# PEER's gate arrays: the one-hot arrays of the first key by eight compare-and-multiply steps on VectorE, and GpSimd as the splitter of the query blocks and the first 17 key blocks only

## The chip, the cores and the metric

The kernel runs on one core of a Trainium2 chip. The time is the device time of one execution of the whole program, in microseconds (us); the median of three runs before the change is 4424.07 us. TensorE (PE in the rows) multiplies matrices, VectorE (DVE), ScalarE (ACT) and GpSimd (POOL) work on arrays in SBUF, and SyncE (SP) issues nearly all DMAs. Each engine takes its own instructions strictly in the order in which the program put them.

## The reference

Three blocks of a network follow one another over 512 tokens of 1024 features. The change lies in the second block's expert layer, PEER. Cut to what matters:

```python
q = einsum('bsd,dk->bsk', xm, w_q).reshape(b, s, 8, 2, 128)      # 8 heads, two keys each
sc = einsum('bshpc,hpnc->bshpn', q, sub_keys)                    # scores of 2 x 128 sub-keys
top_s, top_i = top_k(sc, 16)
best_s, best_c = top_k(top_s[..., 0, :, None] + top_s[..., 1, None, :], 16)   # of 256 pairs
i1, i2 = the two sub-keys of each of the 16 best pairs
g = softmax(best_s)                                              # gates
h = gelu(xm . u[i1 * 128 + i2])                                  # u, v: 16384 x 1024
y = sum over the 8 * 16 chosen experts of g * h * v[i1 * 128 + i2]
```

## The kernel before

The kernel computes all 16384 experts for all tokens and multiplies the hidden values by a dense array of gates that is zero where an expert was not chosen. A block is 128 experts with one second key i2 each for all 128 first keys, or in the kernel's order one key block j: 128 rows of `u` and of `v`. The stage `stage_peer` goes through four stretches.

*Search.* For each of the 8 heads, two query blocks of `peer_w_q` are multiplied with the tokens (`linear`), ScalarE and TensorE make the scores, and `peer_topk` finds the 16 best pairs, all on VectorE. TensorE meanwhile also works through the first of 48 early key blocks of `peer_u` (`EARLY = 48`), whose hidden values ScalarE computes and SyncE stores to DRAM (`H_dr`).

*Gates.* `peer_gates` works on 128 tokens at a time (four times `b`). Three transposes bring i1, i2 and the gates of the chosen pairs onto partitions (`sT`). Then for 8 tokens at a time, 64 units in all, `oa` holds one-hot rows of i2 (a compare of `iot` = 0..127 with `sT`, line 1500) and `oe` one-hot rows of i1 (line 1501) times the gate (line 1502); 8 products on TensorE (line 1506) contract them into the dense gates, ScalarE copies these out of PSUM into `st` (line 1509), and every 32 tokens `st`, 2 MB, is stored to `G_dr` (line 1510). `oa` has two buffers and `oe` three; the products' results take turns in three PSUM banks. In between TensorE goes on with the early key blocks.

*Hand-over.* Key blocks 48 to 51 come next, and are the first whose hidden values are multiplied by the gates at once (`gated`, line 1578): that needs `gt`, loaded from `G_dr` after the last store of `st`. The results, split into `ph` and `pl`, are the moving side of the first products with `peer_v`.

*Groups.* 32 groups of 4 key blocks, with the products for `v` (line 1599).

All big products run in three passes on exact splits of fp32 operands (lines 271 to 273): `whi` is the weights rounded by ScalarE (line 227), `wlo` the rest, a subtraction of two arrays of 128 x 1024 (line 230), on the engine that `linear` is given as `eng`. So a key block is 24 products of 512 columns. Weights as loaded (`wraw`) have three buffers, `whi` and `wlo` two each, so ScalarE rounds block j only once TensorE is through with block j - 2. Query blocks give `wlo` to GpSimd. Of the early key blocks, j <= 20 and the even ones behind them go to GpSimd, the odd ones to VectorE (line 1565).

The order of the instructions on each engine is not the order of the source here: from the attention stage to the end of PEER a scheduler with a simulated timeline places them (`schedule_with_timeline_sim`), with durations of its own. Instructions that cannot run yet hold up all that stand behind them on their engine.

Of the kernel before, what the change touches and what calls it, by code (L numbers as in the profile page):

```python
# [18 lines left out]
OP = mybir.AluOpType  # L19
AX = mybir.AxisListType  # L20
PSUM = bass.MemoryType.PSUM
DRAM = bass.MemoryType.DRAM
# [3 lines left out]
KT = 8  # L26
# [4 lines left out]
# ---------------------------------------------------------------------------  # L31
# host side: layouts only
# ---------------------------------------------------------------------------
# [7 lines left out]
def _blocks_tok(w):  # L41
    """Blocks for products with tokens on the output partitions: [n/256, k half, 128, 4*256]."""
    k, n = w.shape
    return np.ascontiguousarray(
        w.reshape(2, 4, 128, n // 256, 256).transpose(3, 0, 2, 1, 4)
    ).reshape(n // 256, 2, 128, 1024)
# [7 lines left out]
class Layout:  # L54
    """Named columns of the packed per-feature vectors."""
# [16 lines left out]
def host_layout(i):  # L72
    a = {}
# [29 lines left out]
    # block 2  # L103
# [17 lines left out]
    # block 3  # L121
# [23 lines left out]
# ---------------------------------------------------------------------------  # L145
# device side
# ---------------------------------------------------------------------------
# [4 lines left out]
class Ctx:  # L152
# [50 lines left out]
    # -- psum ------------------------------------------------------------  # L203
    def banks(self, es, **split):
        """Share the 8 banks among tags; the tiles of one tag are handed out in order."""
# [14 lines left out]
    # -- exact operand splits ---------------------------------------------  # L220
    def split(self, hi, lo, x, scale=None, eng=None):
        """eng: the engine of lo, or the engines of hi and lo."""
# [18 lines left out]
    def weights(self, src, kt=KT, eng=None, raw=None, pool=None):  # L241
        """One block of up to 128 output columns: [128, kt, 128], split."""
# [8 lines left out]
    def fetch(self, w, blocks, more=(), own=False):  # L251
        """Weights of the first products of the next stage; those of more not split yet.

        own: in a pool of their own, which the next stage closes.
        """
# [10 lines left out]
    def passes(self, ps, terms, first=True, last=True):  # L266
        """terms: (lhs hi, lhs lo, rhs hi, rhs lo); first, last: where the accumulation group starts and ends."""
# [7 lines left out]
    def linear(self, w, blocks, xh, xl, epi, kt=KT, eng=None, front=0, tail=0):  # L275
        """outT[n, t] for each 128-column block of w; epi(j, psum); eng splits the weights.

        The first and the last blocks (front, tail) take one half of the tokens after the other.
        The last ones have epi(j, psum, tokens) and are left to the function returned, of the tokens.
        """  # L280
# [34 lines left out]
    def linear_steps(self, w, blocks, xh, xl, epi):  # L315
        """linear() in steps of KT products of a block."""
# [9 lines left out]
    def linear_tok(self, w, blocks, xh, xl, epi, eng=None):  # L326
        """out[t, n]: tokens on partitions; epi(j, t-pair, psum [128, 2, 256])."""
# [14 lines left out]
    # -- statistics over features ------------------------------------------  # L342
    def colsum(self, s):
        """Sum over partitions, on every partition."""
        ps = self.ax_ps()[:, :s.shape[1]]
        self.nc.tensor.matmul(ps, self.ones, s, start=True, stop=True)
        return ps

    def exp_ln(self, after=None):
        """Load the table set that serves both Exp and Ln."""  # L350
# [3 lines left out]
    def rsqrt(self, *args, load=True, **kw):  # L354
        """out = (scale * ps + eps) ** -0.5, or max(ps, eps) ** -0.5; one Newton step on exp(-ln/2)."""
# [26 lines left out]
    def scratch(self, k, ts, tag):  # L382
        """Room for what is worked out of tile k of x: at the end of a stage, what the stage leaves unused."""
# [13 lines left out]
    def sumsq_ps(self, ps, x, k, ts):  # L397
        """ps accumulates the sum of squares over the features of KT tiles, on every partition."""
# [10 lines left out]
    # -- the ends of stages, in steps between which the halves of the tokens take turns -------  # L409
    def rms_pre(self, g):  # L410
        """What a stage that begins with an RMS norm does with x: its split, scaled by rstd * g."""
# [11 lines left out]
    def modulate_pre(self, scale, shift):  # L423
        """What a stage that begins with a modulation does with x: the split of xt * scale + shift."""
# [10 lines left out]
    def enter(self, xt, pre):  # L435
        """The operands of a stage's first products, unless the stage before has left them."""
# [11 lines left out]
    def leave(self, xt, sums, rest, post, pre, dead, mu=None, first=()):  # L448
        """rest(tokens) and the steps of post(tokens) end a stage, pre begins the next."""
# [18 lines left out]
    def rms_post(self, y, acc, xt, g, sums=None):  # L468
        """xt += rms(y) * g; sums[tokens] = sum of squares of the new xt."""
# [23 lines left out]
class Small:  # L493
    """Arithmetic on small float32 tiles [128, 64]."""
# [85 lines left out]
GH = 8  # L580
# [7 lines left out]
def s5_tables(K, pool, R8, J8):  # L588
    """Discretised poles, their powers with the signs of each half of the partitions, B bar.

    Partitions are (h, n): h = 0 holds real parts of the states, h = 1 imaginary parts.
    """
# [6 lines left out]
    with K.tc.tile_pool(name="s5sm", bufs=1, side="right", reuse_waits="tile") as sp:  # L599
# [54 lines left out]
        # factors of one chunk for the states and for their copy with the halves swapped  # L654
# [6 lines left out]
def s5_inputs(K, u, A_dr, g0):  # L661
    """u: the inputs of the groups from g0 on, a chunk's rows on partitions."""
# [7 lines left out]
def s5_group(K, tb, p1, rot, g0, u, H, G_dr, K_dr):  # L670
    """GH groups: matrices of a chunk of 8 (inputs to states and to outputs), the states each chunk adds."""
# [44 lines left out]
def s5_chunks(K, p2, A_dr, K_dr, Y_dr):  # L716
    """The outputs from within a chunk of 8."""
# [18 lines left out]
def s5_scan(K, tb, rot, H):  # L736
    """The states before each chunk of 8, for every group."""
# [12 lines left out]
def s5_outputs(K, rot, q, H, G_dr, Y1_dr, Y_dr):  # L750
    """GO groups: what the states add to the outputs."""
# [18 lines left out]
def stage_even(K, xt):  # L770
# [9 lines left out]
    with ExitStack() as es:  # L780
# [28 lines left out]
        # conv branch  # L809
# [3 lines left out]
        def conv_pe(j, hb, c):  # L813
            """The taps as products with diagonal matrices."""
# [78 lines left out]
        # S5 branch  # L893
# [1368 lines left out]
```

## Time and profile before

| | |
|---|---|
| three runs | 4424.07 us median, 4422.52 to 4433.23 |
| profiled execution, first to last instruction | 4432.6 us |
| PE busy | 4120.0 us (93%) |
| DVE, ACT, POOL busy | 2799.4, 1756.8, 994.4 us |
| search | about 1541 to 1770 us |
| gates | about 1770 to 2082 us |
| hand-over | about 2082 to 2102 us |
| groups | from 2102 us |

The profiled execution's own time is its span, 4432.6 us; nothing outside the span is recorded for it. It is one execution, and lies near the longest of the three runs. Times in the rows below count from its first instruction. In a row of a group, "x64" is the number of instructions, then come their busy time in us, the mean ns of one, and behind the second bar the idle time of the engine just before them, with what ended it. A row of a timeline begins with the start and the duration; a number in brackets is the idle time before it. Ends of matmuls are modelled, so the step from one start to the next is a better measure of a matmul than its duration.

### The profile page before, as it was taken

Reading aid. Unit: us, or ns where it says so; the run is one execution under the profiler, and the core shown is the slowest. Engines: PE = TensorE matmul, PEld = TensorE weight load, DVE = VectorE, ACT = ScalarE, POOL = GpSimd, SP = SyncE. Lnnn points to the kernel's source line nnn. Section 1 sums busy time; section 2 is a strip of 40 time slices with the busy share of each in tenths; the row PEclk is TensorE's granted clock in tenths of the full one; section 3 lists DMA queues with packets and bytes.
Section 4 is the critical chain, followed back from the end, with each engine's and each line's share of the span. In section 5 each row is a group of like instructions: output and inputs, shape, how many; then the busy total and the mean of one; then the engine's idle time right before and its main releaser. Section 6 shows DMA issues by size and latency. Waiting matters only on the chain.

```text
span 4432.6 us, 54533 instructions
## 1 busy us (share of the span) xinstructions
PE 4120.0 (93%) x20700; PEld 3400.4 (77%) x20700; DVE 2799.4 (63%) x4731; ACT 1756.8 (40%) x2785; POOL 994.4 (22%) x827
## 2 busy tenths in 40 slices
PE   7867897999999899989999999999999999999998
PEld 5656676777776687778888888888877788877887
DVE  8999735555544699997665444444445878735334
ACT  3643634343435522334322322223264444444333
POOL 4855201111021334774000000000023222211000
PEclk9888998999999899999999999999999999999999
DMA  5543533334321123445664434333334222343322
GB/s 149 117 118 116 169 105 117 124 121 136 114 77 53 54 85 127 168 173 202 207 195 140 132 115 128 116 122 119 105 115 149 64 79 70 93 139 109 99 95 86
DMA packets 275062, 532.36 MB, mean 120 GB/s; under 512 B 75968, under 2 KB 149568, under 8 KB 271184
## 3 DMA queue, kind: packets, MB, share of 16 engines
q1 hardware_dynamic: 263328, 505.75, 35.6%
q10 hardware_dynamic: 9216, 9.97, 0.7%
q0 software_dynamic: 2256, 13.17, 0.7%
q8 instruction: 162, 2.65, 0.2%
q14 instruction: 100, 0.82, 0.1%
HBM read 438.11 MB, written 90.70 MB: 119 GB/s over the span
## 4 chain that ended last, share of the span: by engine, by line
PE 49%; DVE 14%; issue 4%; ACT 2%; DMA 2%; POOL 2%; DVEq 0%; SPq 0%; POOLq 0%; ACTq 0%
PE mm L271 14%; PE mm L272 14%; PE mm L273 14%; DVE wlo L230 1%; DVE oa L1500 1%; PE ax L1506 1%; PE z L1225 1%; DVE ti L1435 1%; DVE oe L1501 1%; POOL oe L1502 1%; PE ck L2031 1%; DVE bi L1451 1%; DVE ts L1433 1%; DMA h<-H_dr 1%; DVE wz L1983 0%
## 5 line engine op out<-in xcount | busy, mean ns | idle before, releaser
L271 PE MATMUL mm<-uh,whi 128*128 128x512 f32 (+1 forms) x2888 | 1155.3, 401 | 60.1 <-ACT whi L227 27.0
L273 PE MATMUL mm<-uh,wlo 128*128 128x512 f32 (+1 forms) x2888 | 1131.9, 392 | 53.3 <-DVE wlo L230 49.8
L272 PE MATMUL mm<-ul,whi 128*128 128x512 f32 (+1 forms) x2888 | 1132.3, 392 | 11.3 <-DVE ul L230 9.1
L227 ACT ACTIVATE whi<-wraw 128x1024 fp32r<-128x1024 f32 x455 | 480.3, 1057 | 917.5 <-PE mm L272 650.7
L230 DVE TENSOR_TENSOR wlo<-wraw,whi 128x1024 fp32r<-128x1024 f32 x399 | 515.3, 1293 | 516.5 <-ACT whi L227 504.6
L271 PEld LDWEIGHTS mm<-uh,whi 128*128 128x128 f32 x2888 | 562.8, 195 | 175.6 <-ACT whi L227 31.7
L273 PEld LDWEIGHTS mm<-uh,wlo 128*128 128x128 f32 x2888 | 562.0, 195 | 169.1 <-DVE wlo L230 57.1
L272 PEld LDWEIGHTS mm<-ul,whi 128*128 128x128 f32 x2888 | 563.1, 195 | 120.6 <-DVE ul L230 13.5
L272 PE MATMUL mm<-pl,vh 128*128 128x512 f32 (+1 forms) x1056 | 405.0, 384 | 1.4 <-DVE pl L230 1.4
L273 PE MATMUL mm<-ph,vl 128*128 128x512 f32 (+1 forms) x1056 | 397.7, 383 | 0.0
L271 PE MATMUL mm<-ph,vh 128*128 128x512 f32 (+1 forms) x1056 | 392.8, 384 | 1.9 <-ACT ph L227 1.6
L227 ACT ACTIVATE vh<-wraw 128x1024 fp32r<-128x1024 f32 x128 | 133.1, 1058 | 520.0 <-PE mm L272 320.0
L230 DVE TENSOR_TENSOR vl<-wraw,vh 128x1024 fp32r<-128x1024 f32 x128 | 155.5, 1223 | 190.3 <-ACT vh L227 190.1
L1608 POOL COPY acc<-xt 128x256 f32<-128x256 f32 x2 | 1.9, 961 | 1118.9 <-DVE xt L1606 1118.9
L1603 DVE TENSOR_TENSOR Y<-mm,Y 128x512 f32<-128x512 f32 (+1 forms) x256 | 164.1, 669 | 135.5 <-PE mm L273 135.4
L271 PEld LDWEIGHTS mm<-ph,vh 128*128 128x128 f32 x1056 | 199.2, 189 | 41.1 <-ACT ph L227 1.8
L272 PEld LDWEIGHTS mm<-pl,vh 128*128 128x128 f32 x1056 | 199.2, 189 | 40.8 <-DVE pl L230 2.1
L273 PEld LDWEIGHTS mm<-ph,vl 128*128 128x128 f32 x1056 | 199.3, 189 | 38.7
L1502 POOL TENSOR_TENSOR oe<-oe,sT 128x1024 f32<-128x1024 f32 x64 | 176.5, 2760 | 92.9 <-DVE oe L1501 58.0
L854 POOL TENSOR_TENSOR cvtp<-cvtp,cq 128x512 f32<-128x512 f32 x120 | 174.6, 1456 | 98.6 <-ACT cq L853 93.3
L230 POOL TENSOR_TENSOR wlo<-wraw,whi 128x1024 fp32r<-128x1024 f32 x56 | 154.9, 2771 | 165.7 <-ACT whi L227 165.6
L1506 PEld LDWEIGHTS ax<-oe,oa 128*128 128x128 f32 x1024 | 128.1, 195 | 45.6 <-POOL oe L1502 34.2
(1071 smaller groups left out, 7378.1 us busy)
## 6 DMA issues: line engine op xcount, KB each, us to landing
wraw<-in_peer_u_dram SPq DMA_DIRECT2D x128, 512.0 KB, 3.4
wraw<-in_peer_v_dram SPq DMA_DIRECT2D x128, 512.0 KB, 3.5
wraw<-in_w_in_f_dram SPq DMA_DIRECT2D x66, 512.0 KB, 3.3
G_dr<-st SPq DMA_DIRECT2D x16, 2048.0 KB, 7.5
gt<-G_dr SPq DMA_DIRECT2D x32, 1024.0 KB, 6.8
wraw<-in_w_ffn_dram SPq DMA_DIRECT2D x64, 512.0 KB, 3.3
wraw<-in_w_ada_dram SPq DMA_DIRECT2D x48, 512.0 KB, 3.3
wraw<-in_ev_w_in_dram SPq DMA_DIRECT2D x40, 512.0 KB, 3.4
```

The costliest lines, as they stand in the source:

```text
L227: nc.scalar.activation(out=hi, in_=x, func=AF.Copy)
L230: eng.tensor_tensor(out=lo, in0=x, in1=hi.bitcast(F32), op=OP.subtract)
L271: nc.tensor.matmul(ps, ah, bh, start=first and j == 0, stop=False)
L272: nc.tensor.matmul(ps, ah, bl, start=False, stop=False)
L273: nc.tensor.matmul(ps, al, bh, start=False, stop=last and j == n - 1)
L854: nc.gpsimd.tensor_tensor(out=c, in0=c, in1=t, op=OP.add)
L1225: nc.tensor.matmul(ps[b][:, 128 * (c - b):n], ntri if c == b else nones, at(sp, c, wide[c]), start=False, stop=c == 3, skip_group_check=True)
L1433: v.max(out=ts_[:, x, a:b], in_=src[:, x])
L1435: v.max_index(out=ti[:, x, a:b], in_max=ts_[:, x, a:b], in_values=src[:, x])
L1502: nc.gpsimd.tensor_tensor(out=e, in0=e, in1=sT[:, 2, t0:t0 + 8, None].to_broadcast(sh), op=OP.mult)
L1506: nc.tensor.matmul(pg[:, (r % 4) * 128:(r % 4 + 1) * 128], a[:, r], e[:, r], start=True, stop=True)
L1603: tt(out=Y[:, m, ts], in0=ps, in1=Y[:, m, ts], op=OP.add)
```

## The change

The compare for `oe` on VectorE and the multiplication by the gate on GpSimd, one instruction each for 8 tokens, become 8 instructions on VectorE, one for each token: each compares `iot` with the token's column of i1 and multiplies by the token's column of gates. And GpSimd splits the key blocks j < 17 only; from block 17 on every key block's `wlo` is VectorE's. Comments and docstrings are removed as well, with their lines left empty.

```diff
@@ peer_gates
-                io = iot[:, None, :].to_broadcast(sh)
-                nc.vector.tensor_tensor(out=a, in0=io, in1=sT[:, 1, t0:t0 + 8, None].to_broadcast(sh), op=OP.is_equal)
-                nc.vector.tensor_tensor(out=e, in0=io, in1=sT[:, 0, t0:t0 + 8, None].to_broadcast(sh), op=OP.is_equal)
-                nc.gpsimd.tensor_tensor(out=e, in0=e, in1=sT[:, 2, t0:t0 + 8, None].to_broadcast(sh), op=OP.mult)
+                nc.vector.tensor_tensor(out=a, in0=iot[:, None, :].to_broadcast(sh),
+                                        in1=sT[:, 1, t0:t0 + 8, None].to_broadcast(sh), op=OP.is_equal)
+                for r in range(8):
+                    t = t0 + r
+                    nc.vector.tensor_scalar(out=e[:, r], in0=iot, scalar1=sT[:, 0, t:t + 1], scalar2=sT[:, 2, t:t + 1],
+                                            op0=OP.is_equal, op1=OP.mult)
@@ stage_peer
-    EG, EARLY = 4, 48
+    EG, EARLY, SEARCH = 4, 48, 17
@@
-                         eng=nc.vector if j > 20 and j % 2 else nc.gpsimd)
+                         eng=nc.gpsimd if j < SEARCH else nc.vector)
```

With other durations the scheduler places the instructions anew, between the end of the search and the first groups; everything ahead of and behind that stands in the same order as before. TensorE has 824 big products between the first products with `sk` and the first transposes before the change and 838 now, 663 and then 698 from there to the last product of the gates, and 93 and then 44 from there to the first product with `peer_v`: 1580 in both.

VectorE at the end of the search, before: the last head's work. `cand`, `bi`, `eq` and `slot` are arrays of `peer_topk`, line 1475 is the start of the softmax, on which ScalarE's exponential waits.

```order
L1465 TENSOR_TENSOR eq_12782<-eq_12782,tif_12779 128x2048
L1451 MAX_INDEX bi_12940<-bs_11682,cand_12937 128x8 x2
L1456 MATCH_REPLACE cand_12937<-bs_11682,cand_12937 128x256 x2
L1466 TENSOR_REDUCE slot_11683<-eq_12782 128x8x16
L1456 MATCH_REPLACE cand_12937<-bs_11682,cand_12937 128x256 x2
L1449 MAX bs_11682<-cand_12937 128x8 x4
L1451 MAX_INDEX bi_12940<-bs_11682,cand_12937 128x8 x4
L1475 TENSOR_TENSOR slot_11683<-bs_11682 128x512
```

The same place of the changed kernel; `wlo_15084`, `wlo_15118` and `wlo_15152` are those of key blocks 17, 18 and 19.

```order
L1465 TENSOR_TENSOR eq_12782<-eq_12782,tif_12779 128x2048
L1451 MAX_INDEX bi_12940<-bs_11682,cand_12937 128x8 x2
L230 TENSOR_TENSOR wlo_15084<-wraw_15081,whi_15083 128x1024
L1456 MATCH_REPLACE cand_12937<-bs_11682,cand_12937 128x256 x2
L1466 TENSOR_REDUCE slot_11683<-eq_12782 128x8x16
L1456 MATCH_REPLACE cand_12937<-bs_11682,cand_12937 128x256 x2
L1449 MAX bs_11682<-cand_12937 128x8 x2
L230 TENSOR_TENSOR wlo_15118<-wraw_15115,whi_15117 128x1024
L1449 MAX bs_11682<-cand_12937 128x8 x2
L1451 MAX_INDEX bi_12940<-bs_11682,cand_12937 128x8 x3
L230 TENSOR_TENSOR wlo_15152<-wraw_15149,whi_15151 128x1024
```

The three splits, GpSimd's before, stand among the last head's steps; the first of them stands behind the second half of `bi`. Blocks 20, 21 and 22 follow behind line 1475.

VectorE in the gates, before: the units of 8 tokens.

```order
L1501 TENSOR_TENSOR oe_13017<-iot_11678,sT_12976 128x1024
L230 TENSOR_TENSOR wlo_14904<-wraw_14901,whi_14903 128x1024
L1500 TENSOR_TENSOR oa_13016<-iot_11678,sT_12976 128x1024
L1501 TENSOR_TENSOR oe_13034<-iot_11678,sT_12976 128x1024
L1500 TENSOR_TENSOR oa_13033<-iot_11678,sT_12976 128x1024
```

The same units of the changed kernel.

```order
L1503 TENSOR_SCALAR oe_13029<-iot_11678,sT_12976 128x128 x8
L230 TENSOR_TENSOR wlo_15288<-wraw_15285,whi_15287 128x1024
L1499 TENSOR_TENSOR oa_13028<-iot_11678,sT_12976 128x1024
L1503 TENSOR_SCALAR oe_13052<-iot_11678,sT_12976 128x128 x8
L1499 TENSOR_TENSOR oa_13051<-iot_11678,sT_12976 128x1024
```

The pattern is the same, with 8 small instructions for one large one; GpSimd has nothing left to do here, and twice as many key blocks' `wlo` stand between the units, 30 for 64 units.

ScalarE at the hand-over, before: `st` is the last copy of gates, `whi` and `h` are the rounded weights and the hidden values of key blocks 48 to 51, `vh` the rounded weights of `peer_v`, `ph` the gated hidden values.

```order
L1509 ACTIVATE st_14049<-ax_14112 128x128x4
L227 ACTIVATE whi_15838<-wraw_15836 128x1024
L1532 ACTIVATE h_15795<-mm_15770 128x512
L227 ACTIVATE vh_15909<-wraw_15908 128x1024
L227 ACTIVATE whi_15874<-wraw_15872 128x1024
L227 ACTIVATE vh_15915<-wraw_15914 128x1024
L1532 ACTIVATE h_15831<-mm_15806 128x512
L227 ACTIVATE ph_15760<-h_15795 128x512
```

The same place of the changed kernel.

```order
L227 ACTIVATE whi_16258<-wraw_16256 128x1024
L1534 ACTIVATE h_16215<-mm_16190 128x512
L1511 ACTIVATE st_14409<-ax_14496 128x128x4
L1534 ACTIVATE h_16251<-mm_16226 128x512
L227 ACTIVATE vh_16293<-wraw_16292 128x1024
L227 ACTIVATE vh_16299<-wraw_16298 128x1024
L227 ACTIVATE vh_16305<-wraw_16304 128x1024
L227 ACTIVATE ph_16144<-h_16179 128x512
```

The last copy of gates stood ahead of the last two `whi` and stands behind all of them now: fewer key blocks are left to multiply behind the last gates.

## Rows read from the trace of the kernel before

**Rows 1.** The page: the span, the busy times of its part 1, and the engines of the chain that ended last.

```profile
span 4432.6 us, 54533 instructions
PE 4120.0 (93%) x20700; PEld 3400.4 (77%) x20700; DVE 2799.4 (63%) x4731; ACT 1756.8 (40%) x2785; POOL 994.4 (22%) x827
PE 49%; DVE 14%; issue 4%; ACT 2%; DMA 2%; POOL 2%; DVEq 0%; SPq 0%; POOLq 0%; ACTq 0%
```

**Rows 2.** Two stretches: the gates, and the hand-over with the first group. Columns: from and to, length, busy us and instructions of PE, PEld (weight loads), DVE, ACT and POOL, granted TensorE clock as a share of full speed, DMA share, GB/s.

```profile
1770.00:2082.00 312.00, 280.88 (x1701) 244.52 (x1701) 288.75 (x144) 119.92 (x188) 216.39 (x77) 0.98 0.46 172
2082.00:2140.00 58.00, 56.53 (x249) 46.17 (x248) 28.92 (x36) 24.78 (x35) 0.00 (x0) 1.00 0.81 263
```

**Rows 3.** Groups of instructions by line between 1770 and 2082 us, the four of the gates.

```profile
L1502 POOL TENSOR_TENSOR oe<-oe,sT 128x1024 f32<-128x1024 f32 x64 | 176.5, 2760 | 92.9 <-DVE oe L1501 58.0 <-PE ax L1506 33.7 <-PE mm L273 1.2
L1501 DVE TENSOR_TENSOR oe<-iot,sT 128x1024 f32<-128x1024 f32 x64 | 157.0, 2458 | 0.0
L1506 PE MATMUL ax<-oe,oa 128*128 128x128 f32 x1024 | 133.3, 281 | 31.1 <-POOL oe L1502 26.8 <-DVE oa L1500 4.2
...
L1500 DVE TENSOR_TENSOR oa<-iot,sT 128x1024 f32<-128x1024 f32 x64 | 117.1, 1830 | 18.0 <-ACT sT L1492 14.1 <-PE ax L1506 3.9
```

**Rows 4.** Timelines of GpSimd and VectorE in the gates, from 1809 us on (start, duration).

```profile
1809.45 2.75 POOL L1502 TENSOR_TENSOR oe<-oe,sT 128x1024 f32<-128x1024 f32 x1 [1.23 <-DVE oe L1501]
...
1810.36 2.91 DVE L1500 TENSOR_TENSOR oa<-iot,sT 128x1024 f32<-128x1024 f32 x1
1813.20 1.21 DVE L1501 TENSOR_TENSOR oe<-iot,sT 128x1024 f32<-128x1024 f32 x1
1814.34 1.21 DVE L1500 TENSOR_TENSOR oa<-iot,sT 128x1024 f32<-128x1024 f32 x1
```

**Rows 5.** Timeline of TensorE at the same place: big products around the 8 products of one unit, each of which the trace holds as two records.

```profile
1809.18 0.39 PE L272 MATMUL mm<-ul,whi 128*128 128x512 f32 x1
1809.41 1.95 PE L1506 MATMUL ax<-oe,oa 128*128 128x128 f32 x16
1811.11 0.48 PE L273 MATMUL mm<-uh,wlo 128*128 128x512 f32 x1
1811.42 0.40 PE L271 MATMUL mm<-uh,whi 128*128 128x512 f32 x1
```

**Rows 6.** Other compare-or-scale instructions of VectorE whose scalars are columns of SBUF: timelines of three in a row (one such scalar each, then two each), and the group of the first kind's second half over the whole kernel, most of it beside GpSimd's work.

```profile
397.46 0.67 DVE L825 TENSOR_SCALAR dgh<-ident,wth 128x128 fp32r<-128x128 f32 x3
...
1525.89 1.05 DVE L428 TENSOR_SCALAR oa<-xt,ada 128x256 f32<-128x256 f32 x3
...
L825 DVE TENSOR_SCALAR dgl<-ident,wtl 128x128 fp32r<-128x128 f32 x62 | 25.2, 464 | 0.0
```

**Rows 7.** The end of the search: ScalarE rounding block 18 (as soon as TensorE leaves block 16 for block 17), and VectorE's steps of the last head.

```profile
1739.35 1.06 ACT L227 ACTIVATE whi<-wraw 128x1024 fp32r<-128x1024 f32 x1 [3.89 <-issue]
...
1742.04 0.90 DVE L1459 TENSOR_SCALAR ci<-bi 128x64 uint32<-128x64 uint32 x1
1742.86 0.18 DVE L1460 TENSOR_SCALAR ci<-bi 128x64 uint32<-128x64 uint32 x1
...
1748.54 3.03 DVE L1465 TENSOR_TENSOR eq<-eq,tif 128x2048 f32<-128x2048 f32 x1
...
1751.96 0.41 DVE L1451 FIND_INDEX8 bi<-bs,cand 128x8 uint32<-128x256 f32 x1
...
1760.11 2.29 DVE L1463 TENSOR_TENSOR eq<-cf,iot 128x2048 f32<-128x2048 f32 x1
...
1762.91 3.84 DVE L1465 TENSOR_TENSOR eq<-eq,tif 128x2048 f32<-128x2048 f32 x1
...
1769.08 0.67 DVE L1479 TENSOR_TENSOR slot<-slot,den 128x512 f32<-128x512 f32 x1
```

**Rows 8.** TensorE there: the first product of block 20, two products of block 20 eight steps apart, the first one behind the transposes, and the stretch between 1766 and 1768 us (length, PE busy, granted clock, DMA share, GB/s).

```profile
1761.27 0.80 PE L271 MATMUL mm<-uh,whi 128*128 128x512 f32 x1 [5.46 <-ACT whi L227]
...
1765.25 0.63 PE L271 MATMUL mm<-uh,whi 128*128 128x512 f32 x1
...
1768.66 0.63 PE L273 MATMUL mm<-uh,wlo 128*128 128x512 f32 x1
...
1769.89 0.48 PE L271 MATMUL mm<-uh,whi 128*128 128x512 f32 x1
...
1766.00:1768.00 2.00, 2.00 (x6) 0.50 0.89 261
```

**Rows 9.** The hand-over, on TensorE (the first big product behind the last gates), ScalarE, SyncE, VectorE and TensorE again (the first product with `peer_v`).

```profile
2081.08 0.48 PE L271 MATMUL mm<-uh,whi 128*128 128x512 f32 x1
...
2081.36 0.60 ACT L1509 ACTIVATE st<-ax 128x512 f32<-128x512 f32 x1 [0.29 <-PE ax L1506]
...
2081.99 0.32 SPq L1510 DMA_DIRECT2D G_dr<-st  x1
...
2090.01 3.35 SPq L1574 DMA_DIRECT2D gt<-G_dr  x2
...
2097.86 1.29 DVE L1578 TENSOR_TENSOR h<-h,gt 128x512 f32<-128x512 f32 x2 [2.86 <-DMA gt<-G_dr]
2099.31 1.29 DVE L230 TENSOR_TENSOR pl<-h,ph 128x512 fp32r<-128x512 f32 x2 [0.16 <-ACT ph L227]
...
2102.26 0.39 PE L271 MATMUL mm<-ph,vh 128*128 128x512 f32 x1
```

## The prediction

> **What bounds the kernel now.** I read the page first: TensorE is busy 93% of the span and leads the chain that ended last [rows 1], so a change pays only where TensorE stands still. Then the table of stretches. In the groups TensorE has no gap worth naming. In the gates it is busy 280.9 of 312 us, VectorE 288.8 and GpSimd 216.4 [rows 2]: TensorE loses 31 us there, beside a granted clock of 0.98. Then the groups of that stretch, which say who made it wait: the products of the gates stood 26.8 us for GpSimd's `oe` and 4.2 us for VectorE's `oa` [rows 3]. Last the two timelines, which say why GpSimd is late. VectorE's array instruction takes 1.21 us when GpSimd is idle and 2.91 us when GpSimd runs its 2.75 us multiplication: it ends only behind it [rows 4]. In the groups both of VectorE's instructions are stretched, to means of 1.83 and 2.46 us [rows 3]. So VectorE and GpSimd take turns, a unit of 8 tokens costs 312 / 64 = 4.88 us, and TensorE follows that pace.
>
> **TensorE's own work in the gates.** Between the last gates and the first product with `peer_v` stand 93 big products, which start in 21.18 us (2081.08 to 2102.26 [rows 9]): 0.228 each. A unit's 8 products start at 1809.41, the next big one at 1811.11 and the one behind it 0.31 us later: 1.70 + 0.08 = 1.79 us a unit [rows 5], 64 units 114.6. From the first big product behind the transposes (1769.89 [rows 8]) to the first product with `peer_v` (2102.26 [rows 9]) are 332.4 us, and in them 663 + 93 = 756 big products (172.4 us) and about 1.5 us for nine more transposes. Work: 288.5. Lost: 43.9, of which 31 are the waits, 6 the clock (0.02 of 312), the rest ends of products ahead of a wait, which the trace counts as busy.
>
> **What the change does to it.** GpSimd has no instruction left in the gates, so VectorE's `oa` and its splits fall back to steps of 1.14 us (1813.20 to 1814.34 [rows 4]). The eight new instructions are not in the trace. The nearest rows: three of the same size with one scalar column took 0.67 us, 0.22 each; three of twice the size with two columns 1.05, 0.35 each [rows 6]. I take 0.26, near the first, since the size is the same and a column is added; the bounds are 0.22, and from above the 0.46 mean of the same instruction beside GpSimd's work. Eight are 2.1 us. VectorE's unit is then 1.14 + 2.1 + 30/64 splits of 1.14 (0.53) = 3.8 us. TensorE's is (698 products, 159.1 us, + 114.6 + 1.5) / 64 = 4.30 us. TensorE is the slower, `oe` and `oa` are there ahead of it, and the waits of 31 us and the clock that they cost go. I leave 1.5 us for the first units, behind `sT`, and 4 us for small ones, where a split that waits for ScalarE's rounding holds up the one-hot arrays behind it on VectorE.
>
> [...]
>
> **The hand-over.** The last gates leave TensorE at 2081.08, are copied (2081.36) and stored (2081.99); the load back starts at 2090.01 and is first used at 2097.86; `pl` starts at 2099.31 and takes 0.69, so the first product with `peer_v` could have run at 2100.0 [rows 9], 18.9 us behind the last gates. Before, 93 products (21 us) covered this. Now 44 do: 10.0 us. So TensorE stands 8.9 us where it did not stand; 0 if the 2 MB are stored and read faster, 12 if slower. [...]
>
> **The end of the search.** `wlo` of block 17 was GpSimd's and in time. Now it stands on VectorE behind the index search that ended the step at 1751.96 + 0.33 [rows 7]. Without GpSimd two steps ahead of it lose their stretch: 0.90 to 0.18, and 3.03 to about 2.29 [rows 7], 1.5 us. So the split runs from 1750.8 to 1752.0. But TensorE gets to block 17 at 1739.4 [rows 7], and needs `wlo` for its third product, at 1739.9: it stands 12 us. From 1752.1 it has 22 products of block 17, blocks 18 to 20 and two more, 96 in all, 21.9 us, and 2.8 for the low clock: transposes at 1776.8. VectorE is done a little sooner: 1769.7 [rows 7], 0.3 earlier for block 17 and its gain, three more splits (3.4), less the 1.6 us by which GpSimd's last split stretched it (3.84 to about 2.29), and about 2 us for the rounding of block 20, which waits for block 18 on TensorE: 1773. So the first big product behind the transposes starts at 1777.3 instead of 1769.89: 7.4 us later, with 14 products (3.2 us) more done. Loss: 4.2 us; bounds 1 (VectorE's end decides) and 8 (the clock stays low for two blocks).
>
> **The sum.** Losses in the gates and at the hand-over fall from 43.9 to 1.5 + 4 + 8.9 + 3 = 17.4: a gain of 26.5; the search takes back 4.2. Gain 22 us. The groups behind it hold the same instructions, TensorE is full there (56.5 of 58 us already at their start [rows 2]), so the gain reaches the end. The sum is a difference within the profiled execution, 4432.6 us [rows 1], which lies 8.5 us above the median of the runs; taken from the median, 4424 - 22 = 4402 us. What a measurement of this kernel can tell from no change is about 0.3%, 13 us.
>
> **Rivals.**
> *The hand-over is hidden.* If store and load together take some 9 us less, the wait and its clock go too: 22 + 12 = 34, 4390 us. For it: the new order leaves SyncE few loads in front. Against it: 8.0 us for the store and 7.9 for the load [rows 9], with nothing in the change to shorten them.
> *The waits of the gates stay in smaller form.* VectorE now carries the splits of all key blocks, each behind ScalarE's rounding, itself behind TensorE; two buffers of `oa` let it run ahead by no more than two units. With 0.25 us of waiting in each of the 64 units 16 us are given back: gain 6, 4418 us. For it: half a microsecond of reserve a unit is not much. Against it: the order keeps a whole unit between an array and its use nearly everywhere.
> *VectorE becomes the bound: slower.* The place is the eight instructions. From 0.33 us each VectorE's unit passes TensorE's 4.30; from 0.37 us the gain is gone (22 / 64 = 0.34 us a unit). At the 0.46 of rows 6 a unit is 5.4 us: 64 times 1.1 us, 70 us lost of which the gain covers 22, 4472 us. For it: two columns to fetch and two operations where the cheapest row has one. Against it: the mean of 0.46 was taken beside GpSimd, which is idle now; three in a row without it took 0.22, and with two columns and twice the size 0.35.
>
> **Chances.** The forecast, 4395 to 4410 us by its own bounds (gain 14 to 29): 0.57. Hidden hand-over, 4386 to 4395: 0.13. Smaller gain, 4410 to 4424: 0.20. VectorE the bound: 0.07; 0.03 for a loss from elsewhere. Faster by over 0.3%: 0.57 + 0.13 = 0.70. Within 0.3%: 0.20. Slower: 0.10. The range of 8 in 10 runs from 4388, most of the hidden hand-over, to 4418, most of the smaller gain.
>
> **What would show it.** Right: GpSimd empty in the gates; `oa` at 1.2 us throughout; the new instructions at 0.22 to 0.30 us from start to start; TensorE's waits for `oe` below 5 us; about 4.3 us a unit. A wait of about 12 us on block 17's `wlo` near 1740 us, and one of about 9 us ahead of the first product with `peer_v`. Wrong: steps above 0.33 us or a busy VectorE without gaps, TensorE waiting for `oe` as long as before, or no wait at one of the two places named.

## The result, and the profile after

The changed kernel took 4395.73 us in the median of four runs (4386.04 to 4396.65). The kernel before, run beside it, took 4424.79 us (4422.52 to 4433.23). The ratio is 0.9926, with a 95% interval from 0.9912 to 0.9939: 29 us less, 0.74%, where 22 us had been forecast. Run again later beside three variants, it took 4389.6 us (4387.61 to 4395.25) at a ratio of 0.9909 (0.9892 to 0.9925). The profiled execution took 4396.65 us itself.

The page of the changed kernel, the lines that answer to [rows 1]:

```profile
span 4394.9 us, 54853 instructions
PE 4106.9 (93%) x20700; PEld 3395.0 (77%) x20700; DVE 2749.7 (63%) x5196; ACT 1754.1 (40%) x2785; POOL 766.1 (17%) x746
PE 54%; DVE 11%; issue 3%; ACT 2%; DMA 1%; POOL 1%; DVEq 0%; POOLq 0%; SPq 0%; ACTq 0%
```

The page alone would not tell where the time came from: VectorE has 465 instructions more and is busy 50 us less, and TensorE is busy 93% as before. Stretches tell it. Columns as in [rows 2]:

```profile
1740.00:1760.00 20.00, 11.63 (x44) 9.52 (x45) 19.48 (x43) 3.46 (x4) 0.00 (x0) 0.74 0.31 101
1770.00:2050.00 280.00, 280.00 (x1756) 250.46 (x1756) 240.72 (x606) 121.58 (x192) 0.00 (x0) 1.00 0.53 198
2062.00:2069.00 7.00, 5.82 (x14) 4.56 (x15) 5.38 (x9) 4.82 (x7) 0.00 (x0) 0.53 1.07 367
```

The middle line is the gates: TensorE is busy without a gap at the full clock, GpSimd has no instruction, VectorE is idle for 39 us. Before, TensorE stood 31 us in the gates [rows 3]. The outer lines are the two places where TensorE now stands or runs slowly: the end of the search and the hand-over.

Groups of the gates (1770 to 2050 us), answering to [rows 3]:

```profile
L1503 DVE TENSOR_SCALAR oe<-iot,sT 128x128 f32<-128x128 f32 x512 | 136.5, 343 | 0.0
L1508 PE MATMUL ax<-oe,oa 128*128 128x128 f32 x1024 | 127.2, 274 | 0.0
L1499 DVE TENSOR_TENSOR oa<-iot,sT 128x1024 f32<-128x1024 f32 x64 | 78.2, 1222 | 19.6 <-ACT sT L1492 9.6 <-PE ax L1508 9.6
```

The products of the gates (line 1508, line 1506 before) wait for nobody. The releaser, what ends an idle time, has turned round: it is VectorE that waits, 9.6 us, for TensorE to give back a buffer of `oa`. That is how one sees which of two engines sets the pace. `oa` takes 1.22 us each time, where its mean was 1.83.

VectorE there, start and duration, answering to [rows 4]:

```profile
1796.18 2.14 DVE L1503 TENSOR_SCALAR oe<-iot,sT 128x128 f32<-128x128 f32 x8
1798.24 1.22 DVE L230 TENSOR_TENSOR wlo<-wraw,whi 128x1024 fp32r<-128x1024 f32 x1
1799.37 1.21 DVE L1499 TENSOR_TENSOR oa<-iot,sT 128x1024 f32<-128x1024 f32 x1
```

Eight small instructions take 2.06 us from start to start, 0.257 each. The 0.34 in the group above is the length of one, which overlaps the next: a price per step is read from starts.

The end of the search, on VectorE and TensorE, answering to [rows 7] and [rows 8]:

```profile
1747.11 1.20 DVE L230 TENSOR_TENSOR wlo<-wraw,whi 128x1024 fp32r<-128x1024 f32 x1
...
1748.37 0.80 PE L273 MATMUL mm<-uh,wlo 128*128 128x512 f32 x1 [12.13 <-DVE wlo L230]
1748.96 0.63 PE L271 MATMUL mm<-uh,whi 128*128 128x512 f32 x1
```

TensorE stands 12.13 us for block 17's `wlo`, which VectorE now makes in its turn, and goes on with products of 0.43 us from start to start (six steps from 1748.96 to 1751.52) instead of the 0.23 ahead of the wait: the granted clock is 0.52 from 1748.3 to 1752.

The hand-over, on ScalarE, SyncE, VectorE and TensorE, answering to [rows 9]:

```profile
2047.41 0.60 ACT L1511 ACTIVATE st<-ax 128x512 f32<-128x512 f32 x1 [0.24 <-PE ax L1508]
...
2048.03 0.32 SPq L1512 DMA_DIRECT2D G_dr<-st  x1
...
2055.40 2.10 SPq L1576 DMA_DIRECT2D gt<-G_dr  x2
...
2061.77 1.90 DVE L1580 TENSOR_TENSOR h<-h,gt 128x512 f32<-128x512 f32 x3 [1.82 <-DMA gt<-G_dr]
...
2062.50 1.90 ACT L227 ACTIVATE ph<-h 128x512 fp32r<-128x512 f32 x3 [4.18 <-DVE h L1580]
...
2063.18 2.08 PE L271 MATMUL mm<-ph,vh 128*128 128x512 f32 x4 [5.82 <-ACT ph L227]
...
2065.05 0.63 PE L272 MATMUL mm<-pl,vh 128*128 128x512 f32 x1
```

From the copy of the last gates to the first product with `peer_v` 15.8 us pass, of which TensorE stands 5.82; then 14 steps take 0.43 us each, at a granted clock of 0.50 until 2069. The first product with `peer_v` comes 39.1 us earlier than before, the end of the span 37.7.

### The profile page after: what moved, and what is told of

Read it like the earlier page. It is cut to its first block, busy times and chain, and to the rows that moved or that the text cites. A ratio compares the mean times of both kernels' runs of the same rounds, so it can differ in the third digit from the quotient of the medians.

```text
span 4394.9 us, 54853 instructions
## 1 busy us (share of the span) xinstructions
PE 4106.9 (93%) x20700; PEld 3395.0 (77%) x20700; DVE 2749.7 (63%) x5196; ACT 1754.1 (40%) x2785; POOL 766.1 (17%) x746
## 4 chain that ended last, share of the span: by engine, by line
PE 54%; DVE 11%; issue 3%; ACT 2%; DMA 1%; POOL 1%; DVEq 0%; POOLq 0%; SPq 0%; ACTq 0%
PE mm L271 15%; PE mm L272 15%; PE mm L273 15%; PE ax L1508 3%; PE z L1225 1%; DVE ti L1435 1%; DVE wlo L230 1%; PE ck L2033 1%; DVE ts L1433 1%; DVE bi L1451 1%; DVE wz L1985 0%; DVE bs L1449 0%; PE po L1234 0%; PE z L1207 0%; DVE eq L1463 0%
## 5 line engine op out<-in xcount | busy, mean ns | idle before, releaser
L230 DVE TENSOR_TENSOR wlo<-wraw,whi 128x1024 fp32r<-128x1024 f32 x416 | 530.5, 1277 | 520.1 <-ACT whi L227 509.7
L272 PE MATMUL mm<-wlo,uh 128*128 128x256 f32 x480 | 139.2, 291 | 2.3 <-DVE wlo L230 2.3
L271 PE MATMUL mm<-whi,uh 128*128 128x256 f32 x480 | 137.6, 291 | 1.2 <-ACT whi L227 0.7
L273 PE MATMUL mm<-whi,ul 128*128 128x256 f32 x480 | 138.2, 289 | 0.0
```

Source lines behind the costliest of these rows:

```text
L230: eng.tensor_tensor(out=lo, in0=x, in1=hi.bitcast(F32), op=OP.subtract)
L271: nc.tensor.matmul(ps, ah, bh, start=first and j == 0, stop=False)
L272: nc.tensor.matmul(ps, ah, bl, start=False, stop=False)
L273: nc.tensor.matmul(ps, al, bh, start=False, stop=last and j == n - 1)
```

## Experiments

All times are medians; the ratio is to the kernel before, run beside each.

| variant | us | ratio, 95% interval |
|---|---|---|
| the changed kernel again | 4389.6 | 0.9892 to 0.9925 |
| new one-hot steps, old split rule | 4377.6 | 0.9879 to 0.9912 |
| old one-hot steps, new split rule | 4420.0 | 0.9981 to 1.0000 |
| two large VectorE instructions | 4405.1 | 0.9941 to 0.9975 |
| twelve steps instead of eight | 4445.1 | 1.0031 to 1.0064 |
| GpSimd's work put back, unused | 4493.1 | 1.0133 to 1.0167 |
| blocks 17 to 20 split on GpSimd | 4381.4 | 0.9874 to 0.9907 |
| 52 early blocks | 4384.4 | 0.9879 to 0.9912 |
| the last two together | 4382.8 | 0.9874 to 0.9907 |

**The changed kernel again.** No edit.

> The changed kernel once more, beside three variants of it on the same chip. Every theory expects what its first four executions took, 4386 to 4397 us, a wait of 12 us for block 17's wlo near 1748 us, gates in which TensorE never stands, and a wait of 5.8 us ahead of the first product with peer_v.

Its TensorE waits from 1700 to 2110 us (total, times, longest):

```profile
PE mm L273 <- DVE wlo L230: 7.5, 1, 7.5
PE mm L271 <- ACT ph L227: 6.3, 1, 6.3
```

The time was as expected and so were the gates. The wait for block 17 was 7.5 us and not 12.1; the last section shows why. With the first measurement, eight executions fall into two clusters, four from 4386.0 to 4390.9 and four from 4395.0 to 4396.7. One profile lies in each.

**Half of the change: the eight steps alone.**

```diff
-                         eng=nc.gpsimd if j < SEARCH else nc.vector)
+                         eng=nc.vector if j > 20 and j % 2 else nc.gpsimd)
```

> Half of the change: the eight compare-and-multiply steps, but the splits as before the change (of the early key blocks, 0 to 20 and the even ones on GpSimd). Theory, what counts is that GpSimd's multiplication leaves the gates: 13 splits stay on GpSimd there, each stretching one VectorE instruction by up to 1.7 us (1.21 to 2.91, rows 4), 0.35 us a unit on top of 1.14 + 2.06 + 13/64 x 1.14 = 3.43: 3.8 us, below TensorE's 4.30, so TensorE doesn't stand in the gates. The search is that of the kernel before, and 98 products cover the hand-over: 4382 us (4376 to 4390). Rival, the split rule gives the gain: as the kernel before, 4425. Rival, the splits on GpSimd bring the lock-step back in part: 4400 to 4410, with waits for oe or oa in the gates.

The gates of this variant, columns as in [rows 2]:

```profile
1780.00:2030.00 250.00, 250.00 (x1597) 224.60 (x1597) 228.93 (x550) 111.30 (x176) 29.45 (x12) 1.00 0.54 207
```

TensorE's largest waits from 1700 to 2110 us:

```profile
PE mm L271 <- ACT whi L227: 5.5, 1, 5.5
PE mm L273 <- POOL wlo L230: 2.2, 1, 2.2
```

At 4377.6 us it was within the expectation, 48 us below the kernel before, run beside it. The variant with blocks 17 to 20 split on GpSimd, below, won as much. GpSimd still splits a block a dozen times in the gates, and TensorE never stands: the reserve of VectorE carries it. The waits are those of the kernel before in the search; the changed kernel's wait for `ph` does not come. What such a split costs VectorE, by the timelines of GpSimd and VectorE:

```profile
1782.57 2.38 POOL L230 TENSOR_TENSOR wlo<-wraw,whi 128x1024 fp32r<-128x1024 f32 x1 [12.73 <-ACT whi L227]
...
1782.34 4.23 DVE L1503 TENSOR_SCALAR oe<-iot,sT 128x128 f32<-128x128 f32 x8
...
1787.63 2.13 DVE L1503 TENSOR_SCALAR oe<-iot,sT 128x128 f32<-128x128 f32 x8
```

Eight steps beside it take 4.23 us, the next eight 2.13: of GpSimd's 2.38 us VectorE lost 2.10.

**The other half: the split rule alone**, in the kernel before.

```diff
-                         eng=nc.vector if j > 20 and j % 2 else nc.gpsimd)
+                         eng=nc.gpsimd if j < 17 else nc.vector)
```

> The other half: the kernel before with the new split rule alone (GpSimd splits only query blocks and key blocks 0 to 16), its one-hot arrays still a large compare on VectorE and a large multiplication on GpSimd. Theory: the two engines still take turns, so a unit is at least 2.75 + 1.21 (rows 4) + 26/64 x 1.22 = 4.5 us where it was 4.88, above TensorE's 4.3; up to 24 us are won in the gates if all splits fit in, and 2 to 7 are lost in the search, where the wait for block 17's wlo comes in: 4415 (4405 to 4432), with waits for GpSimd's oe left in the gates. Rival, the split rule gives the whole gain: 4396 or below and no such waits.

TensorE's waits from 1700 to 2110 us:

```profile
PE ax L1506 <- POOL oe L1502: 19.6, 17, 1.5
PE mm L273 <- DVE wlo L230: 12.1, 1, 12.1
PE ax L1506 <- DVE oa L1500: 4.9, 12, 1.6
```

4420.0 us, as expected, and hardly clear of no change. The waits for GpSimd's `oe` stay (19.6 us), the wait of the search comes in. From first to last product of the gates 287.1 us pass, 4.49 a unit, as the sum said. So the gain is the one-hot steps'; the split rule adds nothing to them that the runs show: with it the change won 29 and 40 us, without it 48.

**Two large instructions.** Does the number of VectorE's instructions matter?

```diff
-                for r in range(8):
-                    t = t0 + r
-                    nc.vector.tensor_scalar(out=e[:, r], in0=iot, scalar1=sT[:, 0, t:t + 1], scalar2=sT[:, 2, t:t + 1],
-                                            op0=OP.is_equal, op1=OP.mult)
+                io = iot[:, None, :].to_broadcast(sh)
+                nc.vector.tensor_tensor(out=e, in0=io, in1=sT[:, 0, t0:t0 + 8, None].to_broadcast(sh), op=OP.is_equal)
+                nc.vector.tensor_tensor(out=e, in0=e, in1=sT[:, 2, t0:t0 + 8, None].to_broadcast(sh), op=OP.mult)
```

> The changed kernel with two large VectorE instructions (compare, then multiply, 128 x 1024 each) in place of the eight small ones; nothing on GpSimd. Theory: their number doesn't matter, only that VectorE's unit, 3 x 1.14 + 29/64 x 1.14 = 3.94 us, is below TensorE's 4.3: TensorE does not stand in the gates either. But the order of this variant puts no big product between the last gates and the first one with peer_v, where the changed kernel has 44 (10 us), so the wait there is 15.9 us instead of 5.8: 10 us slower than the changed kernel, 4403 (4396 to 4412). Rival, the eight small ones are what makes the gates fast: waits for oe in the gates, a unit near 4.9 us again, 4425 or above. Rival, fewer instructions are better by themselves: faster than the changed kernel's 4386 to 4397.

The gates of this variant:

```profile
1780.00:2040.00 260.00, 259.53 (x1610) 231.33 (x1608) 229.04 (x199) 110.32 (x172) 0.00 (x0) 1.00 0.52 194
```

TensorE's largest waits from 1700 to 2110 us:

```profile
PE mm L271 <- ACT ph L227: 15.0, 1, 15.0
PE mm L273 <- DVE wlo L230: 7.5, 1, 7.5
PE ax L1507 <- DVE oe L1503: 3.0, 2, 2.5
```

4405.1 us, 2 us from the forecast. The gates are as full as with eight small steps; what this variant loses, it loses at the hand-over, where nothing is left to cover the 15.0 us. Neither the eight instructions nor their number made the gain, but that GpSimd was gone.

**Twelve steps**, the first four of each eight done twice, to find VectorE's limit.

```diff
-                for r in range(8):
+                for r in (*range(8), *range(4)):
```

> The changed kernel with the first four of each eight compare-and-multiply steps done twice (the same values written again), to find where VectorE becomes the bound. Theory: VectorE's unit is 1.14 + 12 x 0.257 + 29/64 x 1.14 = 4.74 us, TensorE's (703 x 0.228 + 116) / 64 = 4.32: 27 us more in the gates; with no big product left behind the last gates 10 us more at the hand-over: 37 us slower than the changed kernel, 4430 (4420 to 4440), and TensorE waits for oe or oa. Rival, VectorE has more reserve than that sum says: only the 10 us of the hand-over, 4403, as the variant with two large instructions.

TensorE's largest wait from 1700 to 2140 us:

```profile
PE ax L1508 <- DVE oe L1503: 27.7, 13, 6.8
```

The groups of `oa` and `wlo` from 1780 to 2110 us:

```profile
L1499 DVE TENSOR_TENSOR oa<-iot,sT 128x1024 f32<-128x1024 f32 x62 | 75.2, 1213 | 13.5 <-ACT sT L1492 10.3 <-PE ax L1508 3.0
L230 DVE TENSOR_TENSOR wlo<-wraw,whi 128x1024 fp32r<-128x1024 f32 x29 | 35.1, 1213 | 8.3 <-ACT whi L227 8.3
```

4445.1 us: slower than before the change, and 5 us above the range. VectorE is the bound, as the sum said, but a unit takes 4.95 us (317 us from first to last product of the gates, over 64) and not 4.74, 64 x 0.21 = 13.4 us in all. The sum left out VectorE's own waits: 13.5 us in front of `oa`, most of it for `sT` at the start of each 128 tokens, and 8.3 in front of `wlo`, for ScalarE's rounding. Against these 21.8 us stand the 9.5 that VectorE had worked on the first units ahead of the first product (1773.06 to 1782.56). So the rival of a slower kernel had its mechanism right. It was at most 0.08 us a step away: VectorE's 39 idle us in the gates of the changed kernel, over 512 steps.

**GpSimd's work put back beside VectorE**, into an array that nobody reads.

```diff
+                for t in (t0, t0 + 4):
+                    z = R.tile([128, 4, 128], F32, name="oz", bufs=1)
+                    nc.gpsimd.tensor_tensor(out=z, in0=iot[:, None, :].to_broadcast([128, 4, 128]),
+                                            in1=sT[:, 2, t:t + 4, None].to_broadcast([128, 4, 128]), op=OP.mult)
```

> The changed kernel with GpSimd's work put back beside VectorE but out of the chain: for each unit GpSimd multiplies 128 x 1024 numbers again, in two halves, into an array that nobody reads. The order on the other engines places the same products (675 in the gates, 44 behind them). Theory, sharing: while GpSimd computes, VectorE hardly gets on (in the variant with the old split rule seven steps beside a split of 2.38 us took 3.97 us instead of 1.87). GpSimd's 128 halves of some 1.4 us, run in four rows of 32 behind each sT, would take 2 to 2.4 us a unit from VectorE: 3.8 + 2.2 = 6.0 us against TensorE's 4.3, some 110 us slower than the changed kernel: 4500 (4460 to 4545), with VectorE's steps stretched and TensorE waiting for oe. Rival, the chain: the loss before was the path VectorE's compare, GpSimd's multiplication, products, one after the other; work of GpSimd that nobody waits for costs nothing: 4386 to 4397, as the changed kernel.

GpSimd and VectorE near the start of the gates (the first line shows 18 instructions as one):

```profile
1779.76 21.06 POOL L1507 TENSOR_TENSOR oz<-iot,sT 128x512 f32<-128x512 f32 x18
...
1785.27 1.21 DVE L1499 TENSOR_TENSOR oa<-iot,sT 128x1024 f32<-128x1024 f32 x1
1786.41 10.01 DVE L1503 TENSOR_SCALAR oe<-iot,sT 128x128 f32<-128x128 f32 x9
```

TensorE's largest waits from 1700 to 2200 us:

```profile
PE mm L273 <- DVE wlo L230: 48.0, 6, 12.1
PE ax L1512 <- DVE oe L1503: 18.7, 30, 1.7
PE ax L1512 <- DVE oa L1499: 12.1, 3, 5.3
```

4493.1 us, 7 us from the forecast and 100 us more than the changed kernel's eight executions (median 4393), although nobody waits for this work. Of the waits above 12.1 us are those of the search; the other 67 lie in the gates, which last 368 us from first to last product instead of 268, at a granted clock of 0.89. The rival as it was put falls: work of GpSimd that nobody waits for was not free. GpSimd's instructions start every 1.17 us (21.06 / 18), and VectorE gets one small step in about each interval (10.01 / 9 = 1.11 us), while a large instruction, of eight times as many numbers, takes 1.14 us there (1785.27 to 1786.41) or 2.0 (1805.30 to 1807.28).

So the 100 us are the price of these many small steps beside GpSimd, and not that of the kernel before. There what the expectation calls sharing shows as stretched instructions of VectorE (2.91 us instead of 1.21 [rows 4]), which was busy 288.8 of 312 us [rows 2] and stood only 3.9 us for TensorE [rows 3]: it was short of time, and the chain from compare to multiplication to product did not hold it up. But no run takes this stretching away and leaves the chain, so that it alone made the 31 us there is argued and not shown; nor does a run show why GpSimd's instructions stretch VectorE's.

**Blocks 17 to 20 split on GpSimd.**

```diff
-    EG, EARLY, SEARCH = 4, 48, 17
+    EG, EARLY, SEARCH = 4, 48, 21
```

> The changed kernel, but key blocks 17 to 20 are split on GpSimd again, as before the change; the gates keep their VectorE splits. Theory: the wait of 12.1 us on block 17's wlo is a loss of TensorE, since its work is the same in sum. It goes, and the kernel before's 5.5 us wait for the rounding of block 20 comes back, so some 4 us are won in the search. The order of this variant has 61 big products between the last gates and the first one with peer_v where the changed kernel has 44; 17 x 0.228 = 3.9 us of the 5.8 us wait go too. Together 8 us: 4388, from 4383 to 4393. Rival, the search ends with VectorE's last steps whatever TensorE does before: then nothing is won there and 4 us at the hand-over: 4392 or above, and TensorE stands as long elsewhere before the transposes.

TensorE's largest waits from 1700 to 2110 us:

```profile
PE mm L271 <- ACT whi L227: 5.5, 1, 5.5
PE mm L273 <- POOL wlo L230: 2.2, 1, 2.2
PE mm L271 <- ACT ph L227: 1.4, 1, 1.4
```

4381.4 us, 1.6 below the range. The waits fell as expected, and the granted clock stayed at 1.00 behind the short wait for `ph` (1.00 from 2050 to 2080 us). But the search itself hardly won: from the last products of the scores to the transposes 119.9 us pass, against 126.1 and 120.4 in the two profiles of the changed kernel, and 14 products fewer (3.2 us) are done in it. That is 3.0 us better than the one and 2.6 worse than the other. Most of the 8 us came from the hand-over.

**52 early blocks.**

```diff
-    EG, EARLY, SEARCH = 4, 48, 17
+    EG, EARLY, SEARCH = 4, 52, 17
```

> The changed kernel with 52 early key blocks instead of 48, nothing else. The order puts 118 big products (27 us) between the last gates and the first product with peer_v instead of 44 (10 us). Theory of the hand-over: last gates to first product took 15.9 us in the changed kernel; 27 us of products cover that, so the wait of 5.8 us goes, and with it the low clock behind it (0.50 for some 6 us, 2 to 3 us of work): 8 us faster, 4388 (4384 to 4391). Rival: the four blocks' hidden values are stored and loaded again, 1 MB each way, which delays the last store of the gates or the loads of gt and h, so that the wait comes back later in the first groups: 4394 to 4400.

TensorE's waits from 1700 to 2110 us:

```profile
PE mm L273 <- DVE wlo L230: 12.1, 1, 12.1
PE mm L271 <- ACT Y L1603: 1.7, 1, 1.7
PE mm L272 <- DVE pl L230: 0.7, 1, 0.7
```

4384.4 us, as expected: the wait for `ph` is gone with its low clock (a granted 1.00 from 2050 to 2100 us); 2.4 us came back as small waits in the first group.

**Both.** [rows 8]'s 5.5 us wait and the covered hand-over in one kernel.

```diff
-    EG, EARLY, SEARCH = 4, 48, 17
+    EG, EARLY, SEARCH = 4, 52, 21
```

> The two edits of the variants before together: 52 early key blocks, and blocks 17 to 20 split on GpSimd. Theory: the two losses lie 280 us apart and add: 4 us from the search and 8 us from the hand-over, 12 us faster than the changed kernel: 4383 (4378 to 4388). Rival, the one hides the other: no faster than the better of the two alone, 4388.

4382.8 us: in the range, but not faster than blocks 17 to 20 alone. The rival is right: that variant had only 1.4 us of the hand-over's wait left to win. Among the last three and the eight steps alone, the intervals overlap; that all four lie below the changed kernel rests on their waits more than on the times.

## Why the prediction was right, and where its terms were off

*The gates* were right in kind and too careful in size. The step was 0.257 us where 0.26 was taken, the clock 1.00, TensorE's unit 4.18 us (267.6 us over 64 from first to last product) where 4.30 was said for a few more products. Counted as the prediction does, from the first big product behind the transposes (1772.13) to the end of the last gates (2047.4), it is 4.30. The term that failed is "I leave 1.5 us for the first units ... and 4 us for small ones": both were 0. Two buffers of `oa` and three of `oe` held VectorE's waits for roundings (9.7 us between 1780 and 2040 us) off TensorE.

The reading of the old gates was too coarse: its 4.88 us a unit is a mean with the splits in it. Where none falls between them, GpSimd's multiplications mostly follow one another in 3.97 us (the next one is the 1809.45 of [rows 4]):

```profile
1801.51 2.75 POOL L1502 TENSOR_TENSOR oe<-oe,sT 128x1024 f32<-128x1024 f32 x1 [1.23 <-PE ax L1506]
1805.48 2.75 POOL L1502 TENSOR_TENSOR oe<-oe,sT 128x1024 f32<-128x1024 f32 x1 [1.22 <-PE ax L1506]
```

With one split of VectorE's between them the step was mostly 5.1 us, with one of GpSimd's mostly 6.0. TensorE's own work was about 4.0 us a unit in that order, an estimate (the 4.18 less the price of 41 big products, 625 instead of 666). So the turns alone about kept up with TensorE, and left no room for the 29 splits of the stretch, 13 on GpSimd and 16 on VectorE. The variant with the old steps and the new split rule agrees: 3.97 us and 28 splits of 1.14 over 64 units make 4.47 of its 4.49.

*The hand-over* was mis-sized: 5.8 us of waiting instead of 8.9. The way from the copy of the last gates to the first product was 15.8 us instead of 18.6: the store was followed by the load after 7.4 us (8.0 before), the load used after 6.4 (7.9), and the first product started 1.4 us behind that instead of 2.1, since it needs `ph` alone, where the prediction had it wait for `pl`. *The low clock* behind it cost 14 steps of 0.43 instead of 0.23 us, 2.8 us; 3 was said. Behind the wait of the search the eight steps from 1748.37 to 1751.89 took 3.52 us instead of 1.82, 1.7 more where 2.8 was said. No run shows the sum's 3 and 2.8 themselves: they are the author's estimates, and the runs showed 2.8 and 1.7 in their place. The variants with 61 and 118 products there (a wait of 1.4 us and none, a granted 1.00 in both) show the hand-over's wait and its low clock to be real and to go with cover.

*The search* was right about the wait, 12.13 us against 12, and not about its constancy: the first big product behind the transposes came 5.9 us later, counted from the last products of the scores, with 14 products (3.2 us) more done, a loss of 2.7 us where 4.2 was forecast. In the other profile of the same kernel the wait was 7.5 us and the same sum gives a gain of 2.9.

*The sum.* From the last products of the scores to the first one with `peer_v` the profiles have 452.8 us before (1649.47 to 2102.26) and 417.4 after (1645.78 to 2063.18): 35.4 us less. The low clock stands behind that and takes 2.8 back, so 32.6 are left, where 22 was forecast. The small waits make 5.5 of the difference, the hand-over and its clock 3.3, the search 1.5: 10.3 of 10.6. TensorE's own work was priced rightly: from the first big product behind the transposes (1772.13) to the first one with `peer_v` are 291.1 us, and 285.2 without the wait, for 742 big products, where the prediction had 288.5 for 756; 14 products are 3.2 us. So the 43.9 us of losses before stand, and every term that was off was set too dear.

3.7 us more lie ahead of the change's first trace, where the order is the same; they are no gain of it. The profiled execution of before was also the longest of its four; the medians give 29 us in the first comparison and 40 in the second, so the size of the gain is known to some 10 us, its sign and place well. That the first median lies within the forecast's own bounds, 4395 to 4410, by 0.7 us, is luck: the second, 4389.6, lies below them, in the range that was given to a hidden hand-over, and by its profile what brought it there is mostly the search (7.1 us better than forecast) and the small waits that did not come (5.5).

*The rivals.* The hidden hand-over was a third right: a third of its wait went. Small waits in the gates were wrong, since the order keeps a whole unit between an array and its use. VectorE as the bound was wrong for eight steps and right for twelve. That fewer instructions on VectorE would decide, a rival of the variant with two large ones, was wrong: eight small ones (2.06 us) even cost less than the two large ones, which go over the numbers twice (2.28, two steps of 1.14 [rows 4]; all VectorE instructions of that variant's gates take 229.04 / 199 = 1.15 in the mean).

## What to carry to other kernels

Work given to GpSimd was not free beside VectorE here: price it at 60 to 90% of its duration on VectorE (1.70 of 2.75 us beside large instructions [rows 4], 2.10 of 2.38 beside small ones; an estimate from these two), and look for it in the mean of VectorE's instructions (`oa` 1.83 us beside GpSimd [rows 3], 1.22 without). Before adding work to an engine beside the bound one, write down the unit of both and VectorE's own waits; the reserve (here 3.7 against 4.2 us a unit) is the whole case. When a stage gets faster, look at what covered the next latency: here the change's first half alone, which left the cover in place, won as much as the whole change with the lost cover mended.

## What had not been expected

The same kernel has two lengths of search. From the last products of the scores to the start of block 17's `wlo` seven profiles show 101.3 us five times (the changed kernel, its variants with 52 blocks, with twelve steps and with GpSimd's work put back, the split rule alone) and 95.3 us twice (the changed kernel again, the two large instructions). VectorE is busy throughout in both. The longer one is the common one: the four kernels that split block 17 on GpSimd, the kernel before among them, show the step below as long and in the same place. The same step in the changed kernel's first profile, with the split of GpSimd beside it, and in its second:

```profile
1709.58 2.40 POOL L230 TENSOR_TENSOR wlo<-wraw,whi 128x1024 fp32r<-128x1024 f32 x1 [3.03 <-ACT whi L227]
...
1710.59 1.47 DVE L1440 CAST tif<-ti 128x128 f32<-128x128 uint32 x1
```

```profile
1702.22 0.22 DVE L1440 CAST tif<-ti 128x128 f32<-128x128 uint32 x1
```

In the first the split started 1 us ahead of this small step and held it up, by 1.25 us, until it was done; in the second none was running. It is one such place of several: counted from the scores the first profile is already 5.3 us behind when this step starts, and 6.0 by block 17. Which steps of VectorE the splits fall on seems to settle in one of two patterns, 6 us apart; what chooses between them was not tried. It would explain the two clusters of times, but with one profile in each that is argued and not shown.
